# Expert weights read as two consecutive rows per partition, in a two-layer diffusion block on one core

## Chip, cores and metric

One core of a Trainium2 chip runs the whole kernel. The metric is the device time of one execution in microseconds; less is better.

## What is computed

Two layers work on 256 latent tokens of 1024 features and on 256 context tokens that share the weights. Each layer modulates its normed input with six vectors from a condition, mixes tokens (attention and a two-directional recurrence, gated and projected), and then runs a mixture of 16 experts, each of which chooses its own 32 tokens per stream. In the last layer the context is no longer needed. All arrays are float32. The part that the change meets:

```python
def expert_choice_ffn(u, w_router, w_gate, w_up, w_down):
    cap = CAPACITY_FACTOR * n // N_EXPERTS          # 32
    aff = jax.nn.softmax((u @ w_router).astype(jnp.float32), axis=-1)
    top_w, top_idx = lax.top_k(jnp.swapaxes(aff, 1, 2), cap)
    xs = jax.vmap(lambda ub, ib: ub[ib])(u, top_idx)
    h = jax.nn.silu(jnp.einsum('becd,edf->becf', xs, w_gate)) * jnp.einsum('becd,edf->becf', xs, w_up)
    y = jnp.einsum('becf,efd->becd', h, w_down) * top_w[..., None].astype(u.dtype)
    ...
```

with `u = layer_norm(x) * (1 + sc2) + sh2`, where `sh2` and `sc2` are sections 3 and 4 of `silu(c) @ w_mod + b_mod`. An expert has three 1024 x 1024 matrices, 12 MB in all; two layers of 16 experts read 403 MB.

## The kernel before

Each layer has a front (`front`: modulation, projections, attention, recurrence, output projection) and a mixture of experts (`moe`). The fronts load some 100 MB in all and are full of products, vector work and small steps. In the mixture the experts run one after the other in a Python loop. For each one `eload` (L994) issues, on SyncE's queue, four transfers of 1 MB for each of the gate, up and down matrices: a tile takes 256 rows of the matrix, row `p` and row `128 + p` of these to partition `p`. `wrow(ts, k)` is the k-th block of 128 rows. The tiles go to a ring of slots (16 in layer 0, 19 in layer 1); a transfer is issued when the product that read the slot before is done. `in_order` keeps the transfers of a layer in the order of the program.

The last expert's down matrix is loaded by `eload_cols` (L1004) in four tiles of 256 columns, with runs of 1 KB, so that the output can be finished quarter by quarter (L1172 to L1182).

Products contract over partitions, so what meets a weight must have its features in the weight's row order. Feature-major columns come from TensorE: `gather` (L1122) loads 128 columns of the normed rows `xh` as the stationary operand and multiplies by the one-hot selection; the rows of the result are modulated with `MT`, the modulation as columns. The hidden rows `h` are transposed at L1219 to meet the down matrix. The router's input is transposed at L1047, and meets the router's weights `wraw`, loaded at L1020 on GpSimd's queue, scaled at L1026 on GpSimd, and multiplied with the shift at L1030. `MT` is made by `mod_cols` (L234) from rows of products, by transposes (L239) and an addition of the bias columns `BM`, which are made once at the start (L225 to L232); layer 0's first two sections come from `mod_first` (L265).

In front of the experts of each layer lie the output projection (L978), its residual and norm (L979, L980, L352 to L359), the router for each tile of 128 tokens (`route`), top-k on VectorE and the first gather. The order of the instructions on an engine is set by a planner that simulates the program with its own costs; `in_order` fixes it where it is written.

Of the kernel before, what the change touches and what calls it, by code (L numbers as in the profile page):

```python
# [19 lines left out]
D = 1024  # L20
KT = D // 128
DEPTH = 2
# [67 lines left out]
def _view(t, offset, pattern):  # L90
    # a strided view of a tile: offset and pattern in elements of one partition
    return bass.AP(tensor=t.tensor, offset=t.offset + offset, ap=[list(t.ap[0])] + pattern)


class HL:
    # a float32 array as the sum of two float32r arrays
# [8 lines left out]
def tile_kernel(ctx, tc, x, c, ctx_in, c_ctx, w_mod, b_mod, w_in, attn_sink, lb_fw, lb_bw, norm_g,  # L105
# [47 lines left out]
    def in_order(chain, ins):  # L153
        # instructions of a chain stay in the order of the program in their engine's queue
        if chain:
            tc.add_manual_dep(ins.ins, chain[0].ins.name,
                              mybir.DependencyInfo(mybir.DependencyClass.NoSync, mybir.DependencyReason.DATA),
                              reason="order")
        chain[:] = [ins]

    def mm3(p, a, b, start, stop, **kw):
        # a^T b in float32 accuracy: the product of the low parts is below its last bit
        mm(p, a.hi, b.hi, start=start, stop=False, **kw)  # L163
        mm(p, a.hi, b.lo, start=False, stop=False, **kw)  # L164
        mm(p, a.lo, b.hi, start=False, stop=stop, **kw)  # L165

    # ---------------------------------------------------------------- constants, small vectors
    # the conditions first: what all else waits on
# [15 lines left out]
    # silu(c), silu(c_ctx) as stationary columns, padded to 32  # L184
# [19 lines left out]
    # lower bounds of the forget gates of the second layer (those of the first are 0): columns (dir, head)  # L204
# [16 lines left out]
    # ---------------------------------------------------------------- modulation, as columns  # L221
    # (section * 2 + half, 128-block, stream); sections 1 and 4 hold 1 + scale
    MT = {l: P.tile([128, 12, 4, 2], F32, name=f"modT{l}") for l in range(DEPTH)}
    BM = P.tile([128, DEPTH, 12, 4], F32, name="bmod")
    brow = t2("brow")[:96, :128]  # L225
    nc.gpsimd.dma_start(brow, _dram(b_mod, 0, [[128, 96], [1, 128]]))
    pt = ob()
    nc.tensor.transpose(pt[:, :96], brow, ident[:96, :96])
    nc.vector.tensor_copy(BM.rearrange("p l q m -> p (l q m)"), pt[:, :96])
# [4 lines left out]
    def mod_cols(l, pm, a, q0, dq, ns):  # L234
        # chunks q0, q0 + dq: quarters of 256 columns, each on the partitions 32 j + stream
        nc.vector.tensor_copy(a, pm[:, 0:256])
        pt = mdb()
        for m in range(2):
            nc.tensor.transpose(pt[:, 128 * m:128 * m + 128], a[:, 128 * m:128 * m + 128], ident)  # L239
# [6 lines left out]
    def mod_first(M0, g):  # L246
        # the shifts and scales of a quarter of the features in layer 0
# [19 lines left out]
    def mod_steps(l, q0, ns):  # L267
        # chunks q0, q0 + 1 of the streams: a step for each 128 rows, whose products take PE's idle times
# [24 lines left out]
    def bcast_rows(l, sec, dst, S, after=()):  # L293
        # dst [128, S, 1024]: section 2 (g1) or 5 (g2), the same on every partition
# [10 lines left out]
    # ---------------------------------------------------------------- layer norm  # L305
# [39 lines left out]
    def ln_affine2(dst, src, lnp, mu, r, seq):  # L345
        # from a pair of banks
# [14 lines left out]
    def transposed(xh, s, k, sink_fn, p):  # L361
        # features [128 k, 128 k + 256) of the two token tiles of a stream, modulated by sink_fn
# [49 lines left out]
    # ---------------------------------------------------------------- token mixers  # L412
    def front(l, fillers, X=None, finish=None):
# [16 lines left out]
        # the last of the fillers wait for PE's idle times in the routing  # L430
# [6 lines left out]
        def filler(f):  # L437
            # the transfer of a step runs a step ahead of its products
# [34 lines left out]
        def cols_tile(*segs, busy=None):  # L473
            # columns of w_in, in one tile of 256
# [10 lines left out]
        def fm(w, j, n, p=None, ks=range(KT)):  # L485
            # features (128 columns j of the tile w) by n tokens
# [5 lines left out]
        # ---- HGRN: one head  # L492
        # axis of directions: 0 backward, 1 forward
# [18 lines left out]
        def hg_chain(h, q, K, F):  # L512
            # decayed scores, keys by queries: AT (within 128 tokens), A1 (tile to tile), A2 (context to x)
# [9 lines left out]
            def sums(Pr, sel, p, start, stop):  # L523
                # sums over features, to each of the 32 keys of a block that sel takes
# [12 lines left out]
            # level 0: a token with itself, both directions  # L537
# [10 lines left out]
            def update(m):  # L548
                # from blocks of m to blocks of 2 m: decay over the other half
# [18 lines left out]
            # levels 1 and 2: products of single pairs, summed over features  # L568
            for i, m in ((1, 1), (2, 2)):
                p = hsb()  # L570
                for j in range(m):
                    Pr = tp("Pr")[:, :TQ]
                    n = TQ // (2 * m)
                    # queries of a second half with key j of the first half (forward)
                    nc.vector.tensor_tensor(_view(Pr, m, [[2 * m, n], [1, m]]), _view(Q, TQ + m, [[2 * m, n], [1, m]]),
                                            _view(K, 512 + j, [[2 * m, n], [0, m]]), op=ALU.mult)
                    # queries of a first half with key j of the second half (backward)
# [5 lines left out]
            # levels 4, 8, 16: blocks of 32 keys by 32 queries; forward keys in first halves, backward in second  # L583
# [17 lines left out]
            # blocks of 32 and of 64 within a tile  # L601
# [23 lines left out]
            # tile to tile: 0 from the second tile to the first (backward), 1 from the first to the second  # L625
# [8 lines left out]
            # context to x, the sum of both directions  # L634
# [33 lines left out]
        # ---- attention  # L668
# [49 lines left out]
        # ---- the schedule of one front  # L718
# [83 lines left out]
        def second(s):  # L802
            # the inputs of the second layer, a stream, in tiles that are free yet; of the context no more is needed
# [57 lines left out]
        else:  # L861
            with ExitStack() as s0:
                xh0 = xh_first(s0)
                M0 = pool(s0, "M0")
                for g in range(5):
# [7 lines left out]
                    # the first head's products as far as the features are there  # L873
                    for i in range(4 if g else 0):
                        fm(ws0[i // 2], i % 2, TQ, ps0[i], range(2 * g - 2, 2 * g))
                # the other constants
# [23 lines left out]
        # ---- branches, gates  # L900
# [59 lines left out]
        # ---- output projection, residual, post norm  # L960
# [11 lines left out]
        # the last token tiles take the first half of w_out first, which is not needed any more then  # L972
# [14 lines left out]
    # ---------------------------------------------------------------- mixture of experts  # L987
    def moe(l, X, M, slots):
# [5 lines left out]
        def eload(src, e):  # L994
            # an expert's matrix in four tiles of 256 rows
            ts = []
            for h in range(4):
                w = next(slots)()
                w = w.rearrange("p (k n) -> p k n", k=2)
                in_order(loads, nc.sync.dma_start(w, _dram(src, (l * NE + e) * D * FF + 256 * h * FF, [[FF, 128], [128 * FF, 2], [1, FF]])))  # L1000
# [3 lines left out]
        def eload_cols(src, e):  # L1004
            # an expert's matrix in four tiles of 256 columns
            ts = []
            for h in range(4):
                w = next(slots)().rearrange("p (k n) -> p k n", k=KT)
                in_order(loads, nc.sync.dma_start(w, _dram(src, (l * NE + e) * D * FF + 256 * h, [[FF, 128], [128 * FF, KT], [1, 256]])))
# [10 lines left out]
        nc.gpsimd.dma_start(wraw[:, :, 0:NE], _dram(w_router, l * D * NE, [[NE, 128], [128 * NE, KT], [1, NE]]))  # L1020
        # the router's weights for the plain norm of a stream: scaled; the shift's share apart
# [12 lines left out]
        def route(s):  # L1034
# [5 lines left out]
            for i in range(2):  # L1040
                t = 2 * s + i
                ln_plain(xh[:, t, :], X[t], i == 0)
                # logits, transposed, in four partial sums; then summed, tokens on partitions
                for h in range(2):
                    p = scb()
                    for m in range(4):
                        nc.tensor.transpose(p[:, 128 * m:128 * m + 128], xh[:, t, 512 * h + 128 * m:512 * h + 128 * m + 128], ident)  # L1047
# [23 lines left out]
            # the taken tokens in their order: 1, 2, ..., the others 0  # L1071
# [11 lines left out]
        def onehot(gi, s):  # L1083
            # the slots of the four experts of a group, as one-hot rows of the tokens
# [8 lines left out]
        def weights(gi, s):  # L1093
            # the weighted one-hot rows of a group, slots on partitions
# [7 lines left out]
            if gi == 3 and s == 0:  # L1102
                # the last expert's rows once more, for every share of its products
# [11 lines left out]
        def gather(gi, s, after=()):  # L1115
            # rows of the four experts of a group, feature-major, modulated
            for k4 in range(0, KT, 4):
                p = tr3() if gi else (ob, acc)[k4 // 4]()
                for k in range(k4, k4 + 4):
                    for i in range(2):  # L1120
                        t = 2 * s + i
                        ins = mm(p[:, 128 * (k - k4):128 * (k - k4) + 128], xh[:, t, 128 * k:128 * k + 128],  # L1122
# [32 lines left out]
        def end_begin():  # L1155
            # the rows of the first stream with all but the last expert's share
# [9 lines left out]
        def end_products(c, py, hT, w, Yc):  # L1166
            # a quarter of the features of the last expert, the blocks of rows in shares
# [7 lines left out]
        def end_first(c, Yc):  # L1175
            # their share of the first stream
# [7 lines left out]
        def end_second(c, Yc):  # L1184
            # the rows of the second one in their place
# [4 lines left out]
        G = 2 if S == 2 else 4          # column groups of the array  # L1190
        MW = 128 // G                   # slots of an expert (both streams)
        NW = FF // G                    # width of a column group's share
        NB = NW // 128
        for gi in range(4):
            for e4 in range(4):
# [22 lines left out]
                for m in range(NB):  # L1218
                    nc.tensor.transpose(pt[:, 128 * m:128 * m + 128], h[:, 128 * m:128 * m + 128], ident)  # L1219
# [19 lines left out]
                if e == 0:  # L1239
                    late = M["late"]()  # L1240
                    Y, g2 = late["Y"], late["g2"]
                    # g2, its stream as the rows of the products of an expert have it
# [36 lines left out]
        def finish_out():  # L1279
            # the output in halves of the rows, one of them on other engines  # L1280
# [29 lines left out]
    def moe_pools(l, st, S, zones, right=()):  # L1310
        # zones: the pools from the bottom, each a list of names of tiles and of numbers of weight slots
# [4 lines left out]
        for z, names in enumerate((right,) + zones if right else zones):  # L1316
            Z = pool(sZ, f"ZR{l}", side="right") if names is right else pool(st, f"Z{l}{z}")
            for n in names:
                if isinstance(n, int):
                    for i in range(n):  # L1320
                        # the place of WM has 1 KB more than its one slot
                        w = 2304 if z == 2 + (right != ()) else 2048
                        slots.append(lambda Z=Z, i=i, w=w: Z.tile([128, w], F32, name=f"w{i}", tag=f"w{i}")[:, :2048])
                elif n not in shapes:
                    # what is not needed before the end of the first expert: a slot until then
                    once.append(lambda Z=Z, n=n: Z.tile([128, 2048], F32, name="w" + n, tag=n))
                    parts.append((n, lambda Z=Z, n=n: Z.tile([128, 2048], F32, name=n, tag=n)))
                else:
                    M[n] = Z.tile([128] + shapes[n], F32, name=n, tag=n)
                    if n == ("xh" if l else "xs"):  # L1330
                        # the place is free when they are loaded
# [19 lines left out]
    with ExitStack() as st:  # L1351
        M, s, once = moe_pools(0, st, 2, ([4], [2], [1], [3], ["g2 OH", 3], ["xh", 3]), ("Y", "xs", "oT"))
        # the slot in the place of the last modulation's weights comes later than the others
        a, b, c = s[7:10] + s[13:16], s[10:13], s[0:6]
        # in the order of release: the second expert's first products come before the first one's last
# [40 lines left out]
```

## Time and profile before

| | us |
|---|---|
| median of 3 runs | 1835.53 (1832.83 to 1835.88) |
| span of the profiled execution, first to last instruction | 1832.6 |
| TensorE busy with products | 1579.6 (86%) |
| VectorE busy | 681.1 (37%) |
| ScalarE busy | 449.7 (25%) |
| GpSimd busy | 304.9 (17%) |
| moved by DMA | 526.06 MB, 287 GB/s on average |

For the profiled execution the page gives the span alone; nothing of what lies around it is shown. Matmuls are pipelined and their ends are modelled, so a busy TensorE is not one at its peak. In the views of DMA a packet is one piece that one of the 16 engines moved; the share is the time of the packets over that of 16 engines.

### The profile page before, as it was taken

How to read it: one execution, taken by the hardware profiler on the slowest of the kernel's cores; microseconds unless marked ns; L12 is line 12 of the kernel's file. 1: busy time of each engine (PE TensorE's matmuls, PEld its weight loads, DVE VectorE, ACT ScalarE, POOL GpSimd, SP SyncE). 2: the span in 40 equal slices, each digit the busy share in tenths (PEclk: the TensorE clock that was granted, in tenths of full speed). 3: DMA queues.
4: the chain of work that ended last, by engine and by line, in shares of the span. 5: the costliest groups of instructions: out<-in, count | busy, mean ns of one | idle time of the engine just before them, and what ended most of it. 6: DMA issues, size and time to landing. Idle time of an engine off the chain costs nothing. (4 is left out here: it accounts for less than half of the span.)

```text
span 1832.6 us, 27361 instructions
## 1 busy us (share of the span) xinstructions
PE 1579.6 (86%) x11339; PEld 921.2 (50%) x11339; DVE 681.1 (37%) x1425; ACT 449.7 (25%) x850; POOL 304.9 (17%) x300
## 2 busy tenths in 40 slices
PE   6999999999989998997988999998968766766675
PEld 4777776688754433332223788775844322322222
DVE  5546566324651211211213756666651110101102
ACT  2436556323120100001001533576410000000000
POOL 2342121224300000000002633331610000000001
PEclk9999999999989999999999999999978866776777
DMA  9544124524679999999999653325689999999997
GB/s 320 183 117 125 60 81 133 202 91 150 258 300 399 409 409 409 409 409 409 409 409 371 213 174 112 122 81 175 239 341 410 409 409 409 409 408 409 409 409 283
DMA packets 207372, 526.06 MB, mean 287 GB/s; under 512 B 9736, under 2 KB 93904, under 8 KB 207248
## 3 DMA queue, kind: packets, MB, share of 16 engines
q1 hardware_dynamic: 205136, 517.46, 75.3%
q0 software_dynamic: 1392, 4.49, 0.7%
q10 hardware_dynamic: 720, 2.36, 0.4%
q8 instruction: 89, 1.46, 0.3%
q14 instruction: 35, 0.29, 0.0%
HBM read 523.23 MB, written 1.05 MB: 286 GB/s over the span
## 5 line engine op out<-in xcount | busy, mean ns | idle before, releaser
L1204 PE MATMUL acc<-w,xs 128*32 128x256 f32 (+1 forms) x3064 | 419.4, 530 | 102.0 <-DMA w<-in_w_up_dram 56.9
L1204 PEld LDWEIGHTS acc<-w,xs 128*32 128x32 f32 (+1 forms) x3064 | 139.1, 134 | 366.5 <-issue 178.1
L1237 PE MATMUL o<-w,hT 128*32 128x256 f32 (+1 forms) x1432 | 196.5, 534 | 43.0 <-DMA w<-in_w_down_dram 29.2
L163 PE MATMUL acc<-uTh,wh 128*128 128x512 f32 (+1 forms) x592 | 215.0, 365 | 2.4 <-ACT sgs L829 1.5
L164 PE MATMUL acc<-uTl,wh 128*128 128x512 f32 (+1 forms) x592 | 212.0, 358 | 0.5 <-DVE uTl L387 0.5
L165 PE MATMUL acc<-uTh,wl 128*128 128x512 f32 (+1 forms) x592 | 210.7, 356 | 0.0
L1215 ACT ACTIVATE h<-acc 128x512 f32<-128x512 f32 (+1 forms) x32 | 15.7, 490 | 534.2 <-PE acc L1204 521.4
L1237 PEld LDWEIGHTS o<-w,hT 128*32 128x32 f32 (+1 forms) x1432 | 65.8, 136 | 153.2 <-issue 74.0
L468 POOL TENSOR_TENSOR wl<-win,wh 128x1024 fp32r<-128x1024 f32 x44 | 113.7, 2584 | 164.0 <-ACT wh L467 162.4
L1216 DVE TENSOR_TENSOR h<-h,acc 128x512 f32<-128x512 f32 (+1 forms) x32 | 17.7, 552 | 308.7 <-PE acc L1204 308.7
L163 PEld LDWEIGHTS acc<-uTh,wh 128*128 128x128 f32 x592 | 111.8, 190 | 27.0 <-issue 7.1
L165 PEld LDWEIGHTS acc<-uTh,wl 128*128 128x128 f32 x592 | 112.3, 190 | 17.7 <-issue 3.4
L164 PEld LDWEIGHTS acc<-uTl,wh 128*128 128x128 f32 x592 | 112.3, 190 | 17.5 <-issue 3.1
L467 ACT CAST wh<-win 128x1024 fp32r<-128x1024 f32 x84 | 84.0, 1046 | 84.3 <-PE acc L164 61.7
L1096 POOL TENSOR_TENSOR OW<-OH,aff 128x256 f32<-128x256 f32 x8 | 4.9, 615 | 598.5 <-PE sc L1219 583.6
L1260 DVE TENSOR_TENSOR Y<-o,g2 OH 32x512 f32<-32x512 f32 x60 | 41.2, 687 | 141.0 <-PE o L1237 140.3
L468 DVE TENSOR_TENSOR wl<-win,wh 128x1024 fp32r<-128x1024 f32 x40 | 53.5, 1338 | 79.7 <-ACT wh L467 78.9
L1221 ACT COPY hT<-sc 128x512 f32<-128x512 f32 (+1 forms) x32 | 15.3, 479 | 256.1 <-PE sc L1219 256.1
L1260 DVE TENSOR_TENSOR Y g<-o,Y g 32x256 f32<-32x256 f32 x60 | 25.2, 420 | 128.0 <-PE o L1237 127.3
L283 PE MATMUL md<-wmod,scol 128*32 128x256 f32 x640 | 57.6, 414 | 6.6 <-DMA wmod<-in_w_mod_dram 5.2
L553 DVE TENSOR_TENSOR K<-K,F 128x512 f32<-128x512 f32 x56 | 46.6, 832 | 8.7 <-PE hs L619 5.3
L322 POOL TENSOR_TENSOR mv<-mv,nhalf 128x1 f32<-128x1 f32 x26 | 24.4, 943 | 130.6 <-DVE mv L321 125.4
(448 smaller groups left out, 2360.1 us busy)
## 6 DMA issues: line engine op xcount, KB each, us to landing
w<-in_w_gate_dram SPq DMA_DIRECT2D x128, 1024.0 KB, 18.6
w<-in_w_up_dram SPq DMA_DIRECT2D x127, 1024.0 KB, 18.5
w<-in_w_down_dram SPq DMA_DIRECT2D x127, 1024.0 KB, 18.6
wmod<-in_w_mod_dram SPq DMA_DIRECT2D x80, 512.0 KB, 4.6
win<-in_w_in_dram SPq DMA_DIRECT2D x26, 1024.0 KB, 6.3
win<-in_w_in_dram SPq DMA_DIRECT2D x32, 512.0 KB, 5.4
wmod<-in_w_mod_dram SPq DMA_DIRECT2D x32, 256.0 KB, 6.2
wo<-in_w_out_dram SPq DMA_DIRECT2D x8, 1024.0 KB, 5.8
```

What stands on the lines that cost most here:

```text
L163: mm(p, a.hi, b.hi, start=start, stop=False, **kw)
L164: mm(p, a.hi, b.lo, start=False, stop=False, **kw)
L165: mm(p, a.lo, b.hi, start=False, stop=stop, **kw)
L283: mm(pm[32 * j:32 * j + 32, 0:256], scol[:, k, :], w[:, 256 * j:256 * j + 256], start=(k == 0), stop=(k == KT - 1))
L322: pows.append(nc.gpsimd.tensor_tensor(mv[:, 2:3], mv[:, 2:3], nhalf[:, 0:1], op=ALU.pow))
L467: nc.scalar.copy(hi[:, r], w[:, r])
L468: ins = eng.tensor_sub(lo[:, r], w[:, r], hi[:, r])
L553: nc.vector.tensor_tensor(kv, kv, _view(f, 0, [[nf + 1, 2], [2, nf // 2], [0, m]]), op=ALU.mult)
L1204: ins = mm(p[MW * j:MW * j + MW, :NW], xs[:, k, e4, :], wrow(w, k)[:, NW * j:NW * j + NW], start=(k == 0), stop=(k == KT - 1))
L1216: nc.vector.tensor_mul(h, h, pu[:, :NW])
L1237: mm(py[MW * dj:MW * dj + MW, :NW], hT[:, 128 * m + MW * j:128 * m + MW * j + MW], wrow(wd, kt)[:, NW * dj:NW * dj + NW], start=(kt == 0), ...
L1260: nc.vector.tensor_tensor(o, py[r:r + 32, :NW], g2[r:r + 32, NW * dj:NW * dj + NW], op=ALU.mult)
```

## The change

`eload` reads rows `2p` and `2p + 1` of its 256 rows to partition `p`, which lie side by side in memory: 8 KB for each partition, where there were two runs of 4 KB. So block `k` of the contraction holds the even (or odd) rows of 256. What meets it follows: `pairs` takes every second column of 256 for the stationary operands of the gather, of the router's transposes and of the hidden rows' transposes; the bias columns of sections 3 and 4 (`6 <= q < 10`) and the transposes of their modulation are taken in that order; the router's weights are loaded in two transfers, even and odd rows; the last expert's column tiles, too, each in two transfers, still with runs of 1 KB. The comments are taken out, so line numbers move.

```diff
+def pairs(v, k):
+    return v[:, 256 * (k // 2) + k % 2:256 * (k // 2) + 256:2]
...
-    brow = t2("brow")[:96, :128]
-    nc.gpsimd.dma_start(brow, _dram(b_mod, 0, [[128, 96], [1, 128]]))
+    brow = t2("brow")[:48, :256]
+    nc.gpsimd.dma_start(brow, _dram(b_mod, 0, [[256, 48], [1, 256]]))
     pt = ob()
-    nc.tensor.transpose(pt[:, :96], brow, ident[:96, :96])
-    nc.vector.tensor_copy(BM.rearrange("p l q m -> p (l q m)"), pt[:, :96])
+    for m in range(2):
+        nc.tensor.transpose(pt[:, 48 * m:48 * m + 48], brow[:, 128 * m:128 * m + 128], ident[:48, :48])
+        nc.tensor.transpose(pt[:, 96 + 48 * m:144 + 48 * m], brow[:, m:256:2], ident[:48, :48])
+    for z, a, b in ((0, 0, 6), (1, 6, 10), (0, 10, 12)):
+        for m in range(2):
+            pv = pt[:, 96 * z + 48 * m:96 * z + 48 * m + 48].rearrange("p (l q j) -> p l q j", l=DEPTH, q=12)
+            nc.vector.tensor_copy(BM[:, :, a:b, m::2], pv[:, :, a:b])
...
     def mod_cols(l, pm, a, q0, dq, ns):
...
-            nc.tensor.transpose(pt[:, 128 * m:128 * m + 128], a[:, 128 * m:128 * m + 128], ident)
+            nc.tensor.transpose(pt[:, 128 * m:128 * m + 128], pairs(a, m) if q0 in (6, 8) else a[:, 128 * m:128 * m + 128], ident)
...
         def eload(src, e):
...
-                in_order(loads, nc.sync.dma_start(w, _dram(src, (l * NE + e) * D * FF + 256 * h * FF, [[FF, 128], [128 * FF, 2], [1, FF]])))
+                in_order(loads, nc.sync.dma_start(w, _dram(src, (l * NE + e) * D * FF + 256 * h * FF, [[2 * FF, 128], [FF, 2], [1, FF]])))
...
         def eload_cols(src, e):
...
-                in_order(loads, nc.sync.dma_start(w, _dram(src, (l * NE + e) * D * FF + 256 * h, [[FF, 128], [128 * FF, KT], [1, 256]])))
+                for i in range(2):
+                    in_order(loads, nc.sync.dma_start(w[:, i::2], _dram(src, (l * NE + e) * D * FF + i * FF + 256 * h,
+                                                                        [[2 * FF, 128], [256 * FF, KT // 2], [1, 256]])))
...
-        nc.gpsimd.dma_start(wraw[:, :, 0:NE], _dram(w_router, l * D * NE, [[NE, 128], [128 * NE, KT], [1, NE]]))
+        for i in range(2):
+            nc.gpsimd.dma_start(wraw[:, i::2, 0:NE], _dram(w_router, l * D * NE + i * NE, [[2 * NE, 128], [256 * NE, KT // 2], [1, NE]]))
...
-                        nc.tensor.transpose(p[:, 128 * m:128 * m + 128], xh[:, t, 512 * h + 128 * m:512 * h + 128 * m + 128], ident)
+                        nc.tensor.transpose(p[:, 128 * m:128 * m + 128], pairs(xh[:, t, :], 4 * h + m), ident)
...
-                        ins = mm(p[:, 128 * (k - k4):128 * (k - k4) + 128], xh[:, t, 128 * k:128 * k + 128],
+                        ins = mm(p[:, 128 * (k - k4):128 * (k - k4) + 128], pairs(xh[:, t, :], k),
...
-                    nc.tensor.transpose(pt[:, 128 * m:128 * m + 128], h[:, 128 * m:128 * m + 128], ident)
+                    nc.tensor.transpose(pt[:, 128 * m:128 * m + 128], pairs(h, m), ident)
```

## Rows read from the trace of the kernel before

**Rows 1.** The page: forty equal slices of the span, in tenths.

```profile
PEclk9999999999989999999999999999978866776777
DMA  9544124524679999999999653325689999999997
```

**Rows 2.** Windows: stretch, length, engines' busy us (instructions), granted clock, DMA share, GB/s.

```profile
core 0: us, PE busy (x) PEld busy (x) DVE busy (x) ACT busy (x) POOL busy (x), PEclk, DMA share, GB/s
530.00:540.00 10.00, 9.45 (x60) 5.34 (x60) 2.31 (x6) 3.57 (x6) 0.00 (x0) 1.00 0.20 61
570.00:580.00 10.00, 10.00 (x50) 4.30 (x48) 1.11 (x2) 0.58 (x1) 0.61 (x1) 1.00 1.02 401
600.00:960.00 360.00, 323.29 (x1451) 113.07 (x1451) 70.09 (x117) 24.56 (x49) 4.41 (x9) 1.00 1.03 409
970.00:980.00 10.00, 9.37 (x44) 2.78 (x44) 0.00 (x0) 0.60 (x1) 0.00 (x0) 1.00 1.03 405
1360.00:1370.00 10.00, 9.86 (x120) 7.88 (x124) 2.25 (x7) 3.49 (x6) 0.00 (x0) 0.85 0.38 134
1410.00:1800.00 390.00, 267.85 (x2568) 101.03 (x2560) 41.93 (x93) 14.93 (x37) 2.36 (x5) 0.73 1.03 409
```

**Rows 3.** The chain that ended last, two pieces of it: start us, us, what.

```profile
1777.28 18.44 DMA w<-in_w_gate_dram
...
1802.55 13.66 DMA w<-in_w_down_dram
```

**Rows 4.** Waits: TensorE from 590 to 980 us, SyncE from 540 to 590; us, times, longest.

```profile
PE acc L1204 <- DMA w<-in_w_up_dram: 9.8, 16, 0.7
PE acc L1204 <- DMA w<-in_w_gate_dram: 6.1, 10, 0.7
...
SPq L1000 <- PE acc L1204: 26.3, 11, 8.2
```

**Rows 5.** DMA from 600 to 960 us: packets, MB, rate.

```profile
DMA packets 38169, 147.30 MB, mean 409 GB/s; under 512 B 2247, under 2 KB 2247, under 8 KB 38154
```

**Rows 6.** DMA from 1808 to 1812 us, the last expert's down matrix.

```profile
DMA packets 1397, 1.41 MB, mean 352 GB/s; under 512 B 23, under 2 KB 1397, under 8 KB 1397
q1 hardware_dynamic: 1397, 1.41, 107.6%
```

**Rows 7.** DMA from 41 to 44.5 us, the constants beside input weights.

```profile
DMA packets 451, 1.41 MB, mean 402 GB/s; under 512 B 43, under 2 KB 177, under 8 KB 450
```

**Rows 8.** DMA from 1318 to 1331 us: GpSimd's queue, two issues with KB and us to landing.

```profile
q0 software_dynamic: 320, 1.11, 21.9%
...
lnp<-in_ln_b_dram POOLq DMA_DIRECT2D x1, 512.0 KB, 11.1
wraw<-in_w_router_dram POOLq DMA_DIRECT2D x1, 64.0 KB, 11.7
```

**Rows 9.** Timeline of layer 1, last projection: start us, us, instruction [idle before <-releaser].

```profile
1331.07 0.76 POOL L1026 TENSOR_TENSOR oT<-wraw,modT 128x128 f32<-128x128 f32 x2 [8.45 <-DMA wraw<-in_w_router_dram]
...
1333.40 1.28 DVE L359 SCALAR_TENSOR_TENSOR X<-X,mv,lnp 128x1024 f32<-128x1024 f32 x1 [0.48 <-POOL mv L322]
...
1334.76 0.70 DVE L979 TENSOR_TENSOR acc<-acc,g1b 128x512 f32<-128x512 f32 x1
```

**Rows 10.** Lines L1020, L1026: ns min/median/max, first and last start in us.

```profile
L1020 POOL DMA_DIRECT2D wraw<-in_w_router_dram x2: 917/918/920, 459.1 to 1319.3; - x2
L1026 POOL TENSOR_TENSOR oT<-wraw,modT x6: 395/400/405, 500.7 to 1331.4; 128x128 f32<-128x128 f32 x6
```

**Rows 11.** The chain that ended last, layer 1's first gather: start us, us, what.

```profile
1360.14 3.39 PE o L1122 x16
1363.53 1.79 PE acc L1122 x16
```

**Rows 12.** Lines L229 and L265 at the start, as in Rows 10.

```profile
L229 DVE COPY bmod<-o x1: 259/259/259, 19.6 to 19.6; 128x96 f32<-128x96 f32 x1
L265 DVE TENSOR_TENSOR modT<-md,bmod x8: 151/156/163, 20.2 to 53.7; 128x4 f32<-128x4 f32 x8
```

## The prediction

> **What bounds the kernel now.** I read the page's forty slices first, then the stages one by one. In the slices the DMA engines are at 9 in two long stretches, and these are the two mixtures of experts; TensorE's clock is 9 in the first and 6 to 8 in the second [rows 1]. The view by windows says the same with numbers: from 600 to 960 us and from 1410 to 1800 us the queue moves 409 GB/s without a gap (a share over 1 means that pieces overlap in their records), while TensorE in the second stretch is busy 268 of 390 us at a granted 0.73, so part of the time at the lower of its levels of 1.2 and 2.4 GHz [rows 2]. The chain of waits agrees: in layer 1 it goes from one weight transfer to the next, some 18 us each, up to the last transfer, which ends at 1816.2 us [rows 3]. In layer 0 TensorE is nearly full, but it still stands 26 times for weights of the gate and up matrices between 590 and 980 us [rows 4]. So a microsecond of transfer saved there is a microsecond of the end, provided the stream is what is late.
>
> That holds not from each layer's first load on. The slots fill, and then the queue waits for the first expert to release them: DMA falls to 0.20 at 530 us and 0.38 at 1360 us [rows 2], and from 540 to 590 SyncE stands 26.3 us for TensorE [rows 4]. Loads that land earlier before that only wait longer. I count the full stream of 4 KB pieces from 575 to 978 us and from 1370 to 1802 us, 403 + 432 = 835 us. After that come the last expert's quarters in 1 KB pieces, which the change leaves at 1 KB.
>
> **The main term: what a piece costs.** The trace has the same sixteen engines full with two sizes of piece. With 4,096 B it moves 409 GB/s [rows 5], or 25.56 GB/s for an engine: 160.2 ns a piece. With 1,024 B, in the tail, it moves 352 GB/s [rows 6], or 22.0: 46.5 ns. The difference, 113.7 ns for 3,072 B, is 0.0370 ns per byte, and 46.5 - 37.9 = 8.6 ns is left as the price of a piece whatever its size. An 8,192 B piece then takes 303.2 + 8.6 = 311.8 ns in place of 2 x 160.2 = 320.4: 2.7% less, 420 GB/s. Over 835 us that is 835 x 8.6 / 320.4 = 22.4 us.
>
> Is a piece of over 4 KB moved as one? No weight load shows it, but the load of the constants (L877) has runs of 5,184 B. In its window [rows 7], 43 of the 451 packets are tiny, 134 have about 1 KB, one is an instruction fetch of some 16 KB, and 273 lie between. The 273 hold 1.41 - 0.137 - 0.016 = 1.257 MB, 4.6 KB on average, more than 4,096, so the long runs were not cut. The formula gives 134 x 46.5 + 273 x 8.6 + 1.257 million x 0.0370 = 55.1 us of engine time, and 16 engines had 16 x 3.5 = 56.0. From 5 KB to 8 KB it is still extrapolated.
>
> The Trainium skill (DMA: Bandwidth & Descriptors, "Why small descriptors are slow") blames about three cycles of an internal bus per packet, which with the 850 MHz of the same page would be an estimate of 3.5 ns. By that the sum would be 835 x 3.5 / 320.4 = 9 us and not 22; the rows at 1 KB and 4 KB show 8.6 ns, so here they differ, and I go by the rows.
>
> **What is added.** (a) Router weights: one load becomes two (L1020), on GpSimd's queue. More than the second issue, its company matters. At 1318 us the two norm vectors and the router's weights (q0: 320 packets, 1.11 MB, about 271 of 4 KB, 17 on each engine) travel beside expert loads, and the router's take 11.7 us to land [rows 8]. Both queues progress at once; if they alternate piece by piece, each of the 17 waits behind 312 ns rather than 160: 17 x 0.152 = 2.6 us later. There is a waiter: GpSimd stands 8.45 us for these weights before L1026, the norm's L322 is queued behind that, VectorE's L359 waits for L322, and on VectorE's queue L979, the last tile of the output projection, starts 0.08 us after L359 ends [rows 9]. So I charge 2.5 us on layer 1's path to routing; the ends are 0 (another order of queues) and 3.5 (the second issue, 0.92 us, comes on top). In layer 0 the same load is issued at 459.1 us and first used at 500.7 [rows 10]: covered, and without that cover the same 2.5 us.
>
> (b) Strided reads by TensorE. The transposes of the router's input (L1047), the gathers (L1122) and the transposes of an expert's hidden rows (L1219) load every second column. Inside the two streams they lie beside transfers. On the path are those ahead of the first expert, 32 + 64 in layer 0 and 16 + 32 in layer 1, and the last experts' 4 + 2: 150 loads. At the low clock 16 pairs of load and product take 3.39 us, 0.212 a pair, in the higher one 1.79 [rows 11]. The load is at most about half of a pair, both being 128 columns, so 0.106 us. No row has a load with a step. The ends: nothing, and a load at half rate, 150 x 0.106 = 15.9 us. A gain has no cause, since no fewer columns are read. I take nothing: a pair's time goes with the clock (3.39 to 1.79), so at step 1 the array and not the read sets it, and the read has some room.
>
> (c) Start: the modulation bias takes four transposes and six copies where there were one and one, ahead of the first columns at 20.21 us, where a copy takes 0.26 us [rows 12]. Five more copies and three more transposes, these at the 0.21 us of a pair at the low clock [rows 11], are at most 5 x 0.26 + 3 x 0.21 = 1.9 us if nothing overlaps; of the eight L265 the last comes at 53.7 us, for a quarter loaded much later, so I put it at nothing. If the first quarter does set the pace, it costs up to 1.9.
>
> (d) The last down matrix is issued in eight halves of a tile, not four tiles. Its engines are full there (107.6%, [rows 6]), so the issues lie under transfers; four more completion marks on each engine, at under 10 ns, are nothing. `mod_cols` changes only an address.
>
> Sum: 22.4 - 2.5 = 19.9 us. Against the profiled execution: 1832.6 - 19.9 = 1812.7 us of span. The median of the runs, 1835.5, lies 2.9 us above that span and moves along: 1815.6.
>
> **Rivals.** *A smaller price per piece.* The 1 KB rate also has rows that are quarter rows 4 KB apart, so part of the 8.6 ns may belong to scattered reads, not to the number of pieces. With half of it: 22.4 / 2 - 2.5 = 8.7 us, 1826.8. For it: the two sizes differ in layout too. Against it: the constants' window fits the formula. The Trainium skill's three cycles (same page and section as above), as an estimate, would end at 1835.5 - 9 + 2.5 = 1829.
>
> *The longer run changes nothing:* the pieces leave at 4 KB, or memory sets the rate. Then only small costs stay, 1835.5 to 1838. For it: the rate is flat at 409 for hundreds of microseconds. Against it: the uncut 5,184 B runs, and the tail, where full engines move less with shorter pieces. The Trainium skill (DMA: Bandwidth & Descriptors, "Specifications") gives about 358 GB/s of memory for a core, by which run length would not matter; the trace's 409 is above it, so this rule doesn't bind here.
>
> *Slower: the strided loads.* Place: the 150 loads ahead of the experts and at the end. If each costs over 19.9 / 150 = 0.133 us more, that is, a load takes over 2.25 times as long, the gain is gone. At four times, 150 x 0.318 = 47.7 us, it ends at 1863. For it: nothing of the kind is in the trace. Against it: a pair follows the clock.
>
> **How the numbers follow.** Forecast, with a gain of 12 to 31 us, 64% (a price per piece of up to 10 ns gives 26 us, and the order of the queues, which a planner sets anew, some 3 to 5 us either way): 1804 to 1823. Smaller price: 10%. Strided loads at half rate, 1831.5: 6%. No effect: 10%. Slower: 10%. The range 1804 to 1832 holds the first three, 80%. About 0.2%, 3.7 us, is what a measurement here can tell from no change: faster 80%, same 10%, slower 10%.
>
> **What would show it.** In both streams some 420 GB/s and about half the packets; 18.0 rather than 18.5 us between the chain's steps; idle DMA ahead of 575 and 1370 us no shorter. The router's weights in layer 1 landing 2 to 4 us later and L979 with them. L1047, L1122 and L1219 with the durations of now. I am wrong if the packets stay at 4 KB, if the rate stays at 409 with longer ones, or if the stretch between the last projection and the first expert grows by more than 4 us.

## The result, and the profile after

The changed kernel takes 1810.2 us (median of 4 runs, 1809.2 to 1812.9), the kernel before on the same chip 1834.5 (4 runs): a ratio of 0.9876, with a 95% interval of 0.9860 to 0.9892, or 22.7 us less (the medians differ by 24.4). The forecast was 1815.6 us and a gain of 19.9. The profiled execution has a span of 1811.2 us, against 1832.6: 21.4 us less.

The page's slices of the kernel after, to be held against [rows 1], with its line of packets:

```profile
PEclk9999999999979999999999999999979777867887
DMA  9644123533679999999999653424689999999997
...
DMA packets 159436, 526.06 MB, mean 290 GB/s; under 512 B 9896, under 2 KB 94064, under 8 KB 111184
```

The shape is the same: two plateaus of DMA at 9, TensorE's clock lower in the second. The next view is DMA from 600 to 950 us of the kernel after, the first stream; it answers [rows 5].

```profile
DMA packets 20232, 147.42 MB, mean 421 GB/s; under 512 B 2248, under 2 KB 2248, under 8 KB 2248
...
w<-in_w_gate_dram SPq DMA_DIRECT2D x48, 1024.0 KB, 19.8
```

Apart from 2,248 tiny ones there is no packet under 8 KB (the tiny ones, 4 bytes and some 9 ns each, are the marks by which each engine tells that its part of a transfer is done): the runs of two rows travel as one piece. The same bytes take 20,232 packets instead of 38,169, and the rate is 421 GB/s instead of 409. By windows, as in [rows 2]:

```profile
core 0: us, PE busy (x) PEld busy (x) DVE busy (x) ACT busy (x) POOL busy (x), PEclk, DMA share, GB/s
530.00:540.00 10.00, 9.39 (x59) 5.77 (x60) 2.89 (x8) 3.90 (x7) 0.00 (x0) 1.00 0.24 79
560.00:570.00 10.00, 10.00 (x50) 4.40 (x49) 2.74 (x4) 0.60 (x1) 0.00 (x0) 1.00 0.80 279
600.00:950.00 350.00, 322.29 (x1455) 117.26 (x1456) 70.00 (x117) 24.70 (x49) 4.42 (x9) 1.00 1.01 421
1350.00:1360.00 10.00, 9.48 (x110) 7.69 (x113) 2.58 (x7) 3.45 (x6) 0.00 (x0) 0.82 0.25 82
1400.00:1780.00 380.00, 253.86 (x2576) 99.79 (x2571) 41.93 (x93) 14.96 (x37) 2.37 (x5) 0.78 1.01 421
```

Both streams are still bound by the transfers: the DMA share stays at 1.01, and TensorE in the second is busy 254 of 380 us. In the first it is busy 322 of 350 us, so there it is not far from being the limit itself. The dips ahead of them are there as before (0.24 at 530 us, 0.25 at 1350).

Where the 21.4 us came from can be read off the first starts of a few lines. Each row below is a stretch between two of them in the profiled executions: the first store of the output projection (L979, after: L990), the first product of an expert (L1204, L1218), the first product with the last down matrix (L1172, L1186). The last two columns are the profiled executions of two experiments told below, the kernel before with only the new loads, and the kernel after with all edits but these.

| stretch | before, us | after, us | difference | only the loads, us | all but the loads, us |
|---|---|---|---|---|---|
| start to the first output projection | 460.7 | 460.6 | -0.1 | 457.6 | 456.4 |
| to the first expert, layer 0 | 73.3 | 74.0 | +0.7 | 73.4 | 73.9 |
| the stream of layer 0 | 452.7 | 441.6 | -11.1 | 440.9 | 452.8 |
| to the output projection of layer 1 | 332.9 | 333.7 | +0.8 | 331.2 | 332.7 |
| to the first expert, layer 1 | 45.6 | 46.0 | +0.4 | 47.3 | 45.6 |
| the stream of layer 1 | 444.6 | 431.8 | -12.8 | 433.0 | 444.3 |
| the last down matrix to the end | 22.8 | 23.5 | +0.7 | 22.5 | 22.3 |

The two streams give 23.9 us, all the rest takes back 2.5. With only the loads the streams are as short as after the change (873.9 us together, for 873.4); with all else they are as long as before (897.1 for 897.3). The other rows are less sure, for each is a single execution: the kernel with only the loads has the code of before in the start, and yet it takes 3.1 us less there. So the 2.5 us are no measured cost of the other edits.

### The profile page after: what moved, and what is told of

It reads as the page before. It is cut to its first block, busy times and chain, and to the rows that moved or that the text cites. A ratio compares the mean times of both kernels' runs of the same rounds, so it can differ in the third digit from the quotient of the medians.

```text
span 1811.2 us, 27388 instructions
## 1 busy us (share of the span) xinstructions
PE 1562.6 (86%) x11342; PEld 925.0 (51%) x11342; DVE 677.1 (37%) x1430; ACT 450.0 (25%) x850; POOL 305.1 (17%) x302
## 3 DMA queue, kind: packets, MB, share of 16 engines
HBM read 523.23 MB, written 1.05 MB: 289 GB/s over the span
## 4 chain that ended last, share of the span: by engine, by line
PE 53%; DMA 37%; DVE 4%; ACT 2%; POOL 2%; issue 1%; SPq 1%; POOLq 0%; ACTq 0%; DVEq 0%
DMA w<-in_w_up_dram 13%; DMA w<-in_w_down_dram 12%; PE acc L168 9%; DMA w<-in_w_gate_dram 9%; PE acc L170 8%; PE acc L169 8%; PE acc L1218 8%; PE o L1251 4%; DMA wmod<-in_w_mod_dram 3%; PE md L294 2%; PE sc L701 2%; PE sc L724 1%; PE o L663 1%; PE tr L719 1%; PE hs L649 1%
## 5 line engine op out<-in xcount | busy, mean ns | idle before, releaser
L1218 PE MATMUL acc<-w,xs 128*32 128x256 f32 (+1 forms) x3064 | 402.9, 512 | 92.0 <-DMA w<-in_w_up_dram 48.9
L1218 PEld LDWEIGHTS acc<-w,xs 128*32 128x32 f32 (+1 forms) x3064 | 138.0, 130 | 339.2 <-issue 175.9
L1251 PE MATMUL o<-w,hT 128*32 128x256 f32 (+1 forms) x1432 | 188.9, 507 | 44.9 <-DMA w<-in_w_down_dram 30.5
L333 POOL TENSOR_TENSOR mv<-mv,nhalf 128x1 f32<-128x1 f32 x26 | 24.4, 942 | 126.7 <-DVE mv L332 126.0
## 6 DMA issues: line engine op xcount, KB each, us to landing
w<-in_w_gate_dram SPq DMA_DIRECT2D x128, 1024.0 KB, 19.8
w<-in_w_up_dram SPq DMA_DIRECT2D x127, 1024.0 KB, 19.8
w<-in_w_down_dram SPq DMA_DIRECT2D x119, 1024.0 KB, 19.8
```

The source lines that it names most:

```text
L333: pows.append(nc.gpsimd.tensor_tensor(mv[:, 2:3], mv[:, 2:3], nhalf[:, 0:1], op=ALU.pow))
L1218: ins = mm(p[MW * j:MW * j + MW, :NW], xs[:, k, e4, :], wrow(w, k)[:, NW * j:NW * j + NW], start=(k == 0), stop=(k == KT - 1))
L1251: mm(py[MW * dj:MW * dj + MW, :NW], hT[:, 128 * m + MW * j:128 * m + MW * j + MW], wrow(wd, kt)[:, NW * dj:NW * dj + NW], start=(kt == 0), ...
```

## Experiments

The theory: a piece has a price of its own, some 9 ns on the engine that moves it, and the change pays it half as often. The first rival: not the number of pieces but their place counts, that is, rows that lie side by side are read faster. The second: the other edits cost something that the sum hid or gave away.

**One part undone: the new order in 4 KB pieces.** Everything as in the kernel after, but each tile is loaded by two transfers, one for each row of the pair.

```diff
-                in_order(loads, nc.sync.dma_start(w, _dram(src, (l * NE + e) * D * FF + 256 * h * FF, [[2 * FF, 128], [FF, 2], [1, FF]])))
+                for i in range(2):
+                    in_order(loads, nc.sync.dma_start(w[:, i], _dram(src, (l * NE + e) * D * FF + (256 * h + i) * FF, [[2 * FF, 128], [1, FF]])))
```

> The changed kernel with each 1 MB load issued as two loads, one for the even and one for the odd rows, so the order of rows and all that follows it is the new one, but the pieces are 4 KB again. Theory (a piece costs some 9 ns whatever its size: 16 engines at 421 GB/s make 311.3 ns for 8 KB, at 409 GB/s 160.2 ns for 4 KB): over some 815 us of full stream 815 x (320.4 / 311.3 - 1) = 24 us are given back, and one more completion mark of 9 ns per MB and engine adds some 3 us: 1837 us. Rival (the neighbouring rows are what is faster to read, not the number of pieces): 1810 to 1814 us, rate 420 GB/s.

Measured: 1836.9 us (median of 10), the kernel before beside it 1832.3 (19 runs); ratio 1.0018, interval 1.0008 to 1.0028. Its DMA from 620 to 940 us:

```profile
DMA packets 35916, 130.93 MB, mean 409 GB/s; under 512 B 3990, under 2 KB 3990, under 8 KB 35901
```

With the new order and old pieces the rate is the old 409, and the whole gain is gone. The order of the rows, and that a transfer's rows are neighbours, give nothing. What the ratio has over 1, 3.3 us (the medians differ by 4.7), may hold the side parts (2 us, below) and the second completion mark of each tile: 3,990 tiny packets, where the kernel with all but the loads has 1,993 in the same window. In the profiled execution its two streams take 898.2 us, 0.9 more than before.

This run also answers a rival that was not named, that the issues and not the pieces were too slow. After the change an issue takes SyncE 0.33 us instead of 2.31 (below); here it takes 0.33 us too (L1012, median), and nothing is gained.

**One part alone: only the loads.** The kernel before, with nothing but the new addresses of `eload`. The work is the same in kind and amount, but the weights' rows meet other features than in the reference.

```diff
-                in_order(loads, nc.sync.dma_start(w, _dram(src, (l * NE + e) * D * FF + 256 * h * FF, [[FF, 128], [128 * FF, 2], [1, FF]])))
+                in_order(loads, nc.sync.dma_start(w, _dram(src, (l * NE + e) * D * FF + 256 * h * FF, [[2 * FF, 128], [FF, 2], [1, FF]])))
```

> The kernel before with the address pattern of the expert loads alone changed (two consecutive rows per partition); everything else stays, so rows meet the wrong features. Theory (the loads are the whole gain, and the strided loads of the stationary operand, the second router load and the bias's copies cost under 1 us): 1809 to 1811.5 us, as the changed kernel. Rival (the rest costs the 2.5 us that the sum had for the router's weights, or more): 1804 to 1808 us.

Measured: 1808.9 us (median of 4), ratio 0.9871, interval 0.9849 to 0.9892, with the rate of the kernel after. Its DMA from 620 to 940 us:

```profile
DMA packets 18496, 134.77 MB, mean 421 GB/s; under 512 B 2055, under 2 KB 2055, under 8 KB 2055
```

The whole change has 0.9876: the two can't be told apart, and between their middles lies 1 us. So the loads are the gain. What the other edits cost is left open: 1808.9 lies between the ranges of theory and rival.

**All but the loads.** The kernel after, with that one line put back (again the features don't match).

> The changed kernel with the address pattern of the expert loads alone put back to rows p and 128 + p; everything else stays changed, so rows meet the wrong features. Theory: all else costs under 1 us, so 1834 to 1836 us, as the kernel before, and 409 GB/s in the stream. Rival (the rest costs 2.5 us or more): 1837 to 1842 us.

Measured: 1835.3 us (median of 10), ratio 1.0011, interval 0.9998 to 1.0024. By the ratio the strided reads, the router's two loads, the bias and the split tail together cost 2 us, and between a gain of 0.4 and a cost of 4.4 is left possible. That is not clear of zero, and it decides neither for the theory (under 1 us) nor for the rival (2.5 or more). Its DMA from 620 to 940 us is at the old rate:

```profile
DMA packets 33924, 130.93 MB, mean 409 GB/s; under 512 B 1993, under 2 KB 1993, under 8 KB 33911
```

**One size changed: 2 KB pieces.** The kernel before, with each tile loaded in two halves of the rows.

```diff
-                in_order(loads, nc.sync.dma_start(w, _dram(src, (l * NE + e) * D * FF + 256 * h * FF, [[FF, 128], [128 * FF, 2], [1, FF]])))
+                for i in range(2):
+                    in_order(loads, nc.sync.dma_start(w[:, :, 512 * i:512 * i + 512], _dram(src, (l * NE + e) * D * FF + 256 * h * FF + 512 * i,
+                                                                                            [[FF, 128], [128 * FF, 2], [1, 512]])))
```

> The kernel before with each 1 MB load issued as two loads of half rows, so its pieces are 2 KB. Theory (some 9 ns per piece): a 2 KB piece takes 75.6 + 9.1 = 84.7 ns, 387 GB/s, in place of 80.1; 835 x 84.7 / 80.1 - 835 = 48 us, and 3 us for more completion marks: 1885 us. Rival (half of the price belongs to scattered short reads in the last expert's tail and does not apply here): about 1860 us, 398 GB/s.

Measured: 1880.5 us in one run, 48 us more than the kernel before beside it (1832.3), and 4.5 us under the theory's 1885. DMA from 620 to 940 us:

```profile
DMA packets 64101, 123.72 MB, mean 387 GB/s; under 512 B 3770, under 2 KB 3770, under 8 KB 64089
```

387 GB/s is 24.2 GB/s for an engine, 84.7 ns a piece of 2 KB: two of them take 9.2 ns more than the 160.2 of one of 4 KB. The same step as from 4 to 8 KB, in the other direction.

**The price by itself.** A kernel that computes nothing and streams transfers of 1 MB on SyncE's queue (2 MB where pieces have 16 KB), each stretch with another size or place of the pieces.

> No block is computed and the output is zero: the queue alone reads expert weights, 24 MB in each of eight ways one after the other. Theory (9 ns per piece, 0.0369 ns per byte and engine, wherever the piece lies): a4 (rows p, 128 + p) 409 GB/s; b8 (rows 2p, 2p + 1 as one piece) 421; c4 (the same rows, a piece for each) 409; d2 (2 KB, neighbouring) 387; e1 (1 KB, neighbouring) 350; f1 (1 KB, 256 columns of 1024 rows) 350; h16 (16 KB) 427; g8 (8 KB of every 64 KB) 421. Rival (where the pieces lie decides): c4 and e1 near b8's 421, g8 near a4's 409.

The DMA line of seven windows, in order: 4 KB, rows 128 apart; 8 KB; 4 KB, rows side by side; 2 KB, neighbours; 1 KB, neighbours; 1 KB, columns of rows 4 KB apart; 8 KB out of every 64.

```profile
DMA packets 3193, 12.29 MB, mean 410 GB/s; under 512 B 192, under 2 KB 192, under 8 KB 3193
...
DMA packets 3012, 21.94 MB, mean 422 GB/s; under 512 B 334, under 2 KB 334, under 8 KB 334
...
DMA packets 5735, 22.12 MB, mean 410 GB/s; under 512 B 336, under 2 KB 336, under 8 KB 5735
...
DMA packets 11288, 22.44 MB, mean 387 GB/s; under 512 B 336, under 2 KB 336, under 8 KB 11287
...
DMA packets 21245, 21.43 MB, mean 357 GB/s; under 512 B 320, under 2 KB 21245, under 8 KB 21245
...
DMA packets 19468, 19.64 MB, mean 357 GB/s; under 512 B 289, under 2 KB 19468, under 8 KB 19468
...
DMA packets 2897, 21.10 MB, mean 422 GB/s; under 512 B 321, under 2 KB 321, under 8 KB 321
```

The size alone sets the rate: 4 KB gives 410 whether the rows lie side by side or 512 KB apart, 1 KB gives 357 in both places, 8 KB gives 422 whether packed or scattered. The 1 KB pieces are faster than the 350 that was expected. At these rates (357, 387, 410, 422 GB/s) a piece of 1, 2, 4 or 8 KB takes 45.9, 84.7, 159.8 or 310.6 ns on its engine. Two pieces of 1, 2 or 4 KB take 7.1, 9.6 or 9.0 ns more than one of twice the size: a price that is paid for each piece, nearly the same from 2 KB up and some 2 ns lower at 1 KB. The Trainium skill (DMA: Bandwidth & Descriptors, "Why small descriptors are slow") has a fixed price per packet too, of about three cycles; the runs here show the fixed price, at two to nearly three times the 3.5 ns that were estimated from that page.

**The router's loads: do two queues share by pieces?** A second kernel without computation. GpSimd's queue loads two vectors of 512 KB (256 pieces of 4 KB) beside a full stream on SyncE's queue, once beside pieces of 4 KB, once of 8, once of 2.

> No block is computed and the output is zero: while SyncE's queue reads 24 MB with 4 KB, then 8 KB, then 2 KB pieces, GpSimd's queue loads two norm vectors of 512 KB, 16 pieces of 4 KB on each engine, in a stream that stays full beyond them. Theory (the queues alternate piece by piece): the vectors' pieces are spread over 16 x (160 + 160) = 5.1 us beside 4 KB, 16 x (160 + 311) = 7.5 us beside 8 KB, 16 x (160 + 85) = 3.9 us beside 2 KB. Rival (the queues share by bytes): 5.1 us in all three.

Measured: from the first to the last of the vectors' pieces, 5.06 us beside 4 KB, 7.45 beside 8 KB and 3.94 beside 2 KB. In that time SyncE's queue moved 253, 255 and 270 pieces. The queues of the window of each:

```profile
q1 hardware_dynamic: 577, 2.23, 69.8%
q0 software_dynamic: 288, 1.05, 33.0%
...
q1 hardware_dynamic: 380, 2.72, 73.0%
q0 software_dynamic: 287, 1.05, 28.8%
...
q1 hardware_dynamic: 680, 1.34, 59.3%
q0 software_dynamic: 288, 1.05, 44.9%
```

GpSimd's 1.05 MB are the same each time (with 32 small pieces); what differs is how much SyncE's queue gets in for each of them. In the order of their starts, 32 of every 64 pieces beside the 8 KB stream are GpSimd's, from beginning to end. So the queues take turns piece by piece, and larger pieces on one slow the other. The Trainium skill (DMA: Bandwidth & Descriptors, "Queues, rings and completion order") says that an engine goes round its queues by packets of some 9 to 17 descriptors; if the 16 engines keep in step, such packets would show as runs of well over a hundred pieces of one queue. Here the longest run is 15 pieces beside the 8 KB stream and 19 at most beside the others, about one for each engine. The records don't name the engine, so the turn of a single engine is inferred from this and not seen.

## Why the prediction was right, step by step

**The main term** was right in mechanism and close in size. The forecast had 8.6 ns a piece from [rows 5, 6] and so 420 GB/s; measured are 9.1 ns (320.4 - 311.3) and 421. The streams gained 11.1 + 12.8 = 23.9 us; the forecast had 22.4, and 835 x 9.1 / 320.4 gives 23.7. The extrapolation from 5 to 8 KB held. Some of the closeness is luck: with the 357 and 410 GB/s of the kernel of piece sizes the same working gives 7.9 ns and 20.6 us; the tail's 352, a little lower, brought the price nearer to that of the larger pieces. The rival "smaller price", which put half of it down to scattered rows, falls with the kernel of piece sizes, where scattered and neighbouring pieces of 1 KB move alike; "no effect" falls with the 421 GB/s of the kernel after.

**The steps of the chain** were forecast at 18.0 us instead of 18.5. They became longer. The chain that ended last, of the kernel after, beside [rows 3]:

```profile
1377.05 19.82 DMA w<-in_w_down_dram
1396.94 19.80 DMA w<-in_w_up_dram
...
1765.06 19.89 DMA w<-in_w_up_dram
1787.90 9.83 DMA w<-in_w_down_dram
```

The misreading: such a step runs from the issue of a transfer to its landing, past all transfers that lie ahead of it in the queue, and not from one landing to that of the next transfer. A transfer of 1 MB takes 2.56 us at 409 GB/s and 2.49 at 421, so 18.6 us (the median from issue to landing of L1000) are 7.3 transfers and 19.8 are 8.0. Below are the issues (ns min/median/max) and, from 1410 to 1760 us, the largest group of SyncE's waits (us in total, times, longest), first of before, then of after:

```profile
L1000 SPq DMA_DIRECT2D w<-in_w_gate_dram x128: 367/2310/4612, 453.0 to 1777.3; - x128
...
SPq L1000 <- PE acc L1204: 113.4, 59, 4.5
```

```profile
L1011 SPq DMA_DIRECT2D w<-in_w_gate_dram x128: 327/328/1290, 452.9 to 1755.1; - x128
...
SPq L1011 <- DMA w<-in_w_up_dram: 103.5, 48, 3.6
```

Before, SyncE was held for 2.31 us at each issue, about the time that a transfer takes to move, and waited in between for products to free a slot. After, an issue takes 0.33 us, and in front of each of its 139 issues in that stretch SyncE waits some 2.1 us for an earlier transfer to land (48 times for one of the up matrix, 91 for gate and down). That is the depth of 8.0: the transfers of this queue use eight semaphores in turn, and an issue waits for its own, which the transfer eight places ahead raises when it lands. The kernel with the new order in 4 KB pieces, whose transfers are half as large, fits this too, with 10.2 us from issue to landing, eight times 1.28. None of this sets the pace: the engines were full in both kernels.

**(a) The router's weights** were mis-sized, at 2.5 us. The timeline of the kernel after, for [rows 9]:

```profile
1321.71 1.79 POOL L1040 TENSOR_TENSOR oT<-wraw,modT 128x128 f32<-128x128 f32 x2 [8.16 <-DMA wraw<-in_w_router_dram]
...
1324.07 1.28 DVE L370 SCALAR_TENSOR_TENSOR X<-X,mv,lnp 128x1024 f32<-128x1024 f32 x1 [0.84 <-POOL mv L333]
1325.28 0.69 DVE L990 TENSOR_TENSOR acc<-acc,g1b 128x512 f32<-128x512 f32 x1
```

All of it stands 9.3 to 9.5 us earlier than before, and the first L990 of this layer 9.7 (1309.9 for 1319.6): 0.2 to 0.4 us were lost here and not 2.5. The alternation is as forecast, the sharing kernel shows it. But the sum took SyncE's queue to be full all along. DMA from 1308 to 1321 us, as in [rows 8]:

```profile
q1 hardware_dynamic: 455, 3.33, 70.7%
q0 software_dynamic: 352, 1.11, 22.6%
...
lnp<-in_ln_b_dram POOLq DMA_DIRECT2D x1, 512.0 KB, 12.2
wraw<-in_w_router_dram POOLq DMA_DIRECT2D x2, 32.0 KB, 11.5
```

Here SyncE has only 3.33 MB to move beside 1.11, before as after: three expert transfers, issued by 1308.7 us, and the next one finds a slot only at 1318.8 us (before: 1318.4 and 1328.5). Whichever queue is served more often, the engines are done with both at about the same time, and the router's weights come last. The pieces of the kernel after show it: from 1313 to 1319 us the two queues start about as many (196 and 195, marks left out), and from 1319 to 1320 it is 69 of GpSimd's and 19 of SyncE's, whose three transfers are nearly used up, so that GpSimd's rest no longer has to take turns. The router's weights landed 11.5 us after their issue, for 11.7; the vector ahead of them took 12.2 instead of 11.1. What the forecast should have read from [rows 8] is the bytes on both queues until SyncE's next issue, not the time of a piece.

**(b) Strided reads** were put at nothing, and on the path that nearly held, though not for the reason given. What a step of 2 costs depends on the clock. Line L1219 before and L1233 after, the transposes of the hidden rows, most of them at the high clock (ns min/median/max):

```profile
L1219 PEld LDWEIGHTS sc<-cst,h x96: 137/141/229, 549.6 to 1808.6; 128*128 128x128 f32 x96
L1219 PE MATMUL sc<-cst,h x96: 272/273/473, 549.6 to 1808.8; 128*128 128x128 f32 x96
```

```profile
L1233 PEld LDWEIGHTS sc<-cst,h x96: 194/209/223, 550.1 to 1786.8; 128*128 128x128 f32 x96
L1233 PE MATMUL sc<-cst,h x96: 272/288/488, 550.1 to 1786.9; 128*128 128x128 f32 x96
```

The load goes from 141 to 209 ns, 1.5 times, and the product from 273 to 288. The claim was that the array and not the read sets a pair's time, so that the read has room. At the low clock that held: with 0.50 granted, the eight transposes of the first tile that the router sees in layer 1 take 1.98 us before (L1047, from 1342.75) and 2.00 after (L1061, from 1333.26). At the high clock it did not: the read got slower, and the pairs with it. Layer 1's first gather, in the chain of the kernel after, of which the second row has the full clock (1.00 granted) in both kernels:

```profile
1350.67 3.45 PE o L1136 x16
1354.12 1.88 PE acc L1136 x16
```

Beside 3.39 and 1.79 [rows 11] these are 0.15 us for 32 pairs; over 150 pairs that would be 0.7 us, an estimate. The stretch ahead of layer 0's first expert, where 96 of the 150 lie, agrees with it: 73.9 to 74.2 us in the three profiled executions with the step, 72.1 to 73.4 in the three without. The rival "slower" wanted over 133 ns a pair; it got 5. The bound that it was worked out from, a load of at most half a pair or 0.106 us, was wrong: in the first half of that gather a load before the change is recorded with 333 ns (median) while a pair takes 212, so loads and products overlap.

**(c) The start** was put at nothing: the first columns come at 19.6 us (L276), for 20.2 [rows 12], and the first output projection 0.1 us earlier than before. As that stretch takes anything from 456.4 to 460.7 us in the profiled executions, with or without these edits, it can't exclude the 1.9 us; that the columns come no later speaks against them.

**(d) The split tail** was put at nothing as well. The stretch behind it is 0.7 us longer in the table, but the split is not the cause. The products with the last down matrix, of the kernel after and of the kernel with all but the loads, which has the same split:

```profile
L1186 PE MATMUL o<-w,hT x64: 379/518/636, 1787.7 to 1798.5; 128*32 128x256 f32 x64
```

```profile
L1186 PE MATMUL o<-w,hT x64: 379/497/635, 1805.8 to 1815.4; 128*32 128x256 f32 x64
```

10.8 us there, 9.6 here, and 10.0 before without a split; from the first of these products to the end the kernel with all but the loads takes 22.3 us, the least of the four in the table. The difference goes with the clock: from 1788 to 1793 us of the kernel after,

```profile
1788.00:1793.00 5.00, 4.46 (x34) 2.11 (x27) 0.85 (x2) 0.00 (x0) 0.00 (x0) 0.50 1.02 345
```

TensorE has 0.50 of its clock, the level of 1.2 GHz, while the matching windows, behind the first of these products, have 0.65 before and 0.60 in the kernel with all but the loads. In the 5 us ahead of these it is the other way round, 0.91 in the kernel after and 0.50 in the two others: the stretch at the low clock comes later there. Why was not tested.

**The sum.** What the forecast took off, 2.5 us, is what the table shows for all that is not stream, but by accident: it was all put on the router, where at most 0.4 us lie. Of the rest, 0.7 us lie ahead of layer 0's first expert and go with the step (b). The 0.8 in layer 1's front and the 0.7 in the tail have no cause that a run here shows: over the profiled executions of the six kernels that compute the block, these stretches take 331.2 to 333.7 us and 22.3 to 24.4 us, and the change edits nothing between L1186 and the output projection but an address in `mod_cols`. And the median was set 2.9 us above the profiled span, of which only some 1.75 us lie outside the span (each of the later runs is that much longer than its own span: 1812.9 to 1811.2); the other 1.15 would be the difference between that execution and the median one. It shifts the forecast by about 1 us.

## What to carry to other kernels

Where the engines of DMA are full, count the pieces of a stretch and take the price of one from two sizes in the same trace; lay out the contraction so that a partition's rows are neighbours in memory, and let the stationary operands follow with a step. Read a landing time as a depth of the queue, and judge a shared load by the bytes on all queues until the next issue. Pieces of 16 KB, in the kernel of piece sizes, moved 430 GB/s (410 to 445 us), 1.9% above the 422 of 8 KB there; a version with four rows per partition needs slots of twice the size and was not tried, and in layer 0 TensorE, busy 322 of 350 us, could soon be the limit.

## What the runs showed of the hardware beyond that

- At 1, 4 and 8 KB the rate of a full stream did not depend on where the pieces lie: neighbours or columns of scattered rows (357 GB/s), neighbours or rows 512 KB apart (410), packed or one of every 64 KB (422).
- In a full stream an issue of 1 MB held SyncE about as long as the transfer takes to move: 2.3 us with pieces of 4 KB (median, both kernels), and in the kernel of piece sizes 2.6 us with 2 KB and 2.8 with 1 KB. With 8 KB it took 0.33 us, and SyncE waited for an earlier landing instead.
- At the high clock a stationary load of 128 contiguous float32 columns for a transpose took 141 ns, with step 2 it took 209. The loads of the gathers (L1122, L1136), with the selection as moving operand, took 192 ns (median) contiguous and 196 with the step, and their products 275 and 281. At the low clock the step cost next to nothing: 1.98 and 2.00 us for eight transposes.
